# Four cached tiles of DSA per transfer, and one transposed-probability tile for two heads, in a two-layer streaming encoder step

## The chip, the cores and the metric

The kernel runs on one NeuronCore of a Trainium2 chip. The metric is device time in microseconds, the median of 3 runs. Times inside a run come from one profiled execution; a time such as 1469.76 is microseconds from that execution's first instruction.

Engines are called as in the profile: PE (matrix multiply), DVE (vector), ACT (scalar), POOL (GpSimd), SP (it issues nearly all loads and stores here). Each engine works through its own list in order and waits on semaphores of the others.

## The reference

Two layers of a streaming encoder, for a prompt of 512 rows and 8 running streams of 16 rows (640 rows, f32). Two of a layer's four branches are attention, and only those are touched:

```python
def mla_attend(q_pos, qb, k, v, k_pos):            # branch A, 4 heads
    s = jnp.einsum('bqhd,bshd->bhqs', qb, k).astype(F32) * A_SCALE
    s = jnp.where(vis[None, None], s, -jnp.inf)
    p = jax.nn.softmax(s, axis=-1).astype(v.dtype)
    return jnp.einsum('bhqs,bshd->bqhd', p, v)

def dsa_attend(...):                               # branch B, 4 heads
    _, sel = lax.top_k(iscore, topk)               # an indexer chooses the keys
    logits = jnp.einsum('bqhd,bqkhd->bqhk', qb, k_sel).astype(F32) * B_SCALE
    logits = logits + jnp.moveaxis(bias, -1, 2)
    p = jax.nn.softmax(logits, axis=-1).astype(v.dtype)
    return jnp.einsum('bqhk,bqkhd->bqhd', p, v_sel)
```

The streams attend over 512 cached rows each beside their own 16. The cached keys and values of branch B come as `c_bkT` (2 layers, 4 heads, 4 tiles of 128 x 512) and `c_bv` (2 layers, 2 head pairs, 8 streams, 128 x 512); a tile is 256 KB.

## The kernel before

**Order.** The code is written as a plain sequence. A scheduler that estimates when each operation can start sets the order on every engine at build time; on the chip that order is fixed. So between the small matmuls of attention stand matmuls of the gate projections (lines 117 to 119, 128 x 320 each, three to a product), which depend on no attention and fill PE.

**Attention of the prompt.** One unit is a block of 128 queries (`qt` 0 to 3) and a pair of heads. `mla_front` and `dsa_front` make scores and softmax and leave `P`, one tile for each head. `mla_back` and `dsa_back` turn `P`: `transposed` puts up to four 128 x 128 blocks of one head into a PSUM bank (line 680) and copies the bank to an SBUF tile `PT` with `cp`, which takes ACT and DVE in turn (lines 96, 98). Then `pv` (line 728) multiplies with the values: for each key block one matmul for each of the two heads. The two heads write PSUM rows 0 to 63 and 64 to 127 and use two different 64-column groups of the PE array (`tile_position=(0, 64 * hf)`). There are 80 of these in MLA and 80 in DSA over both layers, 160 in all. `piped` lets the fronts run two units ahead of the backs.

**Attention of the streams in DSA.** `dsas_front(h)` loads four tiles of `c_bkT`, each into a buffer of its own (`cache()`, tag `ca`, 4 buffers, shared with other uses), and makes one score matmul from each (line 916), each on its own 32-column group and 32 PSUM rows (`tile_position=(0, 32 * p)`): 32 over both layers. `dsas_back` does the values for two heads: for each half of the streams (`g` 0 and 1) four tiles of `c_bv` (tag `cd`, 4 buffers) and 16 matmuls (line 952) that go round the four 32-column groups: 128 over both layers. Line 935 transposes, line 942 is the product with the streams' own rows.

**Loads.** SP issues all these loads in its own fixed order, with the gate weights (`wst`, 512 KB each) among them. A load waits in that list until its buffer is free, and all that stands behind it waits too.

A matmul of f32 operands shows as two rows in the trace, a transposition or a projection matmul as one.

Of the kernel before, what the change touches and what calls it, by code (L numbers as in the profile page):

```python
# [22 lines left out]
NT = 5  # L23
NJ = 22
REG = 3
DFF = 2816
ALPHA = (2 * L) ** 0.25
EPS = 1e-5
# [227 lines left out]
def layer(tc, l, I, O, E):  # L256
# [4 lines left out]
    xh, xl, ident = E["xh"], E["xl"], E["ident"]  # L261
# [31 lines left out]
    def cache():  # L293
        return mk(at, "ca", 512, 4)
# [400 lines left out]
    def pt(nm, p, n, w=T):  # L695
        return mk(p, nm, w, n)

    def piped(units, front, back, lag):
        held = []
        for u in units:  # L700
            held.append((u, front(*u)))
            if len(held) > lag:
                v, r = held.pop(0)
                back(*v, r)
        for v, r in held:
            back(*v, r)
# [14 lines left out]
            out.append(P)  # L721
        return out

    def pv(po, PTs, v, n, h0):
        for kb in range(n):
            for hf, PT in enumerate(PTs):
                o = kb * 256 + 64 * (h0 + hf)
                pe.matmul(po[64 * hf : 64 * hf + 64], lhsT=v[:, o : o + 64], rhs=PT[:, kb * 128 : kb * 128 + 128],  # L728
                          start=kb == 0, stop=kb == n - 1, tile_position=(0, 64 * hf))

    def mla_back(qt, k, Ps):
        PTs = [transposed(P, qt + 1, pt("PT", m2, 3, 512)) for P in Ps]
        if k == 0:
            mla[qt] = aps()
        po = mla[qt][:, k * 128 : k * 128 + 128]
        pv(po, PTs, va, qt + 1, 2 * k)
        split_out(0, k, slice(qt * 128, qt * 128 + 128), po)
# [168 lines left out]
    def dsas_front(h):  # L906
        k, hf = h // 2, h % 2
        ns = slice(64 * hf, 64 * hf + 64)
        cb = mk(ds, "cb", T, 2)
        sp.dma_start(cb, biasS[h])  # L910
        pool.tensor_tensor(cb, cb, wk[3], op=ALU.add)
        ps, pn = aps(), aps()[:, 0:128]
        for p in range(4):
            c_ = cache()
            sp.dma_start(c_, I["c_bkT"][l, h, p])
            pe.matmul(ps[32 * p : 32 * p + 32, :], lhsT=db[:, h * 128 + 32 * p : h * 128 + 32 * p + 32], rhs=c_,  # L916
                      start=True, stop=True, tile_position=(0, 32 * p))
        pe.matmul(pn, lhsT=bq[k][ns], rhs=bk[k][ns], start=True, stop=True)
        P = pt("P", ds, 4)
        sm = col()  # L920
        dsa_soft([(ps, 512), (pn, 128)], cb, P, sm)
        norm(P, T, sm)
        return P

    def dsas_back(h, P):
        k, hf = h // 2, h % 2
        if hf == 0:
            dsa["s", k] = mk(ds, "PT2", 5 * 256, 1)
        PT = dsa["s", k]
        PTv = PT.rearrange("p (b s f q) -> p b s f q", b=5, s=NS, f=2)  # L930
        for b in range(5):
            if b % 4 == 0:
                ps = aps()
            tp = ps[:, (b % 4) * 128 : (b % 4) * 128 + 128]
            pe.transpose(tp, P[:, b * 128 : b * 128 + 128], ident)
            cp(PTv[:, b, :, hf], s3(tp))
        if hf == 0:
            return
        pr = aps()[:, 0:256]
        for g in range(2):  # L940
            pg_ = pr[:, g * 128 : g * 128 + 128]
            pe.matmul(pg_, lhsT=PT[:, 1024 + g * 128 : 1152 + g * 128], rhs=bv[:, 1024 + k * 128 : 1152 + k * 128],
                      start=True, stop=False)
            cs_ = []
            for i in range(4):
                c_ = mk(ds, "cd", 512, 4)
                sp.dma_start(c_, I["c_bv"][l, k, 4 * g + i])
                cs_.append(c_)
            for kb in range(4):
                for i, c_ in enumerate(cs_):  # L950
                    o = kb * 256 + g * 128 + i * 32
                    pe.matmul(pg_[32 * i : 32 * i + 32], lhsT=PT[:, o : o + 32], rhs=c_[:, kb * 128 : kb * 128 + 128],
                              start=False, stop=kb == 3, tile_position=(0, 32 * i))
        pc_ = mk(ds, "cb", T, 2)[:, 0:256]
        act.copy(pc_, pr)
        po = aps()[:, 0:256]
        for g in range(2):
            pe.transpose(po[:, g * 128 : g * 128 + 128], pc_[:, g * 128 : g * 128 + 128], ident)
        pov = po.rearrange("p (s f q) -> p s f q", s=NS, f=2)
        for f in range(2):  # L960
            rows = slice(64 * f, 64 * f + 64)
            hi = s3(bh[1][k][rows, TP:T])
            act.copy(hi, pov[rows, :, f])
            dve.tensor_sub(s3(bl[1][k][rows, TP:T]), pov[rows, :, f], hi.bitcast(F32))
# [32 lines left out]
        return out  # L997

    def dsa_back(k, qt, Ps):
        PTs = [transposed(P, qt + 1, pt("PT", ds, 4, 512)) for P in Ps]  # L1000
        if qt == 0:
            dsa[k] = aps()
        pv(dsa[k][:, qt * 128 : qt * 128 + 128], PTs, bv, qt + 1, 2 * k)
        if qt == 3:
            split_out(1, k, slice(0, TP), dsa[k])
# [465 lines left out]
```

## Time and profile before

| | |
|---|---|
| median of 3 runs | 2123.42 us (2122.09 to 2124.9) |
| the profiled execution | 2131.17 us, of which its span from first to last instruction 2128.8 us |
| PE busy | 2069.5 us, 97% of the span |
| DVE, ACT, POOL busy | 72%, 43%, 22% |
| chain of work that ended last | PE 80%, DVE 7%, DMA 5% |

The page has the busy time of each engine, the span in 40 slices, the queues, and the chain followed back from the last instruction. A matmul's time from start to end overlaps with the next one's; what a matmul costs PE is the step from its start to the next start.

Attention and the projections between stand at about 257 to 505 us (layer 0) and 1307 to 1564 us (layer 1) of the span.

### The profile page before, as it was taken

The page shows a single profiled execution, that of the slowest core. Times are in us where ns is not written, and L with a number is a line of the kernel's source. Part 1 is how long each engine was busy: PE and PEld are TensorE (multiplying, and loading weights), DVE is VectorE, ACT ScalarE, POOL GpSimd, SP SyncE. Part 2 cuts the span into 40 slices and gives each one's busy share as a digit, 9 for nine tenths or more (in the row PEclk, how much of TensorE's full clock was granted, in tenths as well). Part 3 has the DMA queues.
Part 4 walks back from the last instruction along what each step waited for, and adds up shares of the span by engine and source line. Part 5 has one row for each costly group of instructions (what it writes and reads, how often), then busy time and mean ns, then how long its engine had stood idle before and what let it go on. Part 6 is the DMA issues. An engine that isn't in the chain of part 4 may idle for free.

```text
span 2128.8 us, 33842 instructions
## 1 busy us (share of the span) xinstructions
PE 2069.5 (97%) x12828; PEld 1863.3 (88%) x12828; DVE 1533.4 (72%) x2775; ACT 913.8 (43%) x1682; POOL 459.6 (22%) x709
## 2 busy tenths in 40 slices
PE   6999999999999999999899999999999999999997
PEld 6998979779989899989699999797898899899995
DVE  6999994633389778766679989945334899679657
ACT  5433432322256545544434334333232566555543
POOL 2200001411114323322302000023110143323222
PEclk9999999999999999999999999999999999999999
DMA  8452225432443544542653522254324344525525
GB/s 275 105 166 85 75 72 162 136 126 80 144 141 112 117 106 103 129 120 70 175 144 82 171 64 71 92 166 132 107 85 150 136 123 120 128 89 140 129 54 152
DMA packets 137882, 257.22 MB, mean 121 GB/s; under 512 B 33068, under 2 KB 53328, under 8 KB 137200
## 3 DMA queue, kind: packets, MB, share of 16 engines
q1 hardware_dynamic: 121880, 223.61, 33.0%
q0 software_dynamic: 15840, 31.46, 8.7%
q8 instruction: 101, 1.65, 0.3%
q14 instruction: 61, 0.50, 0.1%
HBM read 202.06 MB, written 52.96 MB: 120 GB/s over the span
## 4 chain that ended last, share of the span: by engine, by line
PE 80%; DVE 7%; DMA 5%; issue 4%; ACT 3%; POOL 2%; SPq 0%; DVEq 0%; POOLq 0%; ACTq 0%
PE g L118 18%; PE g L117 18%; PE g L119 18%; PE a L117 5%; PE a L118 5%; PE a L119 5%; PE a L728 1%; PE a L680 1%; DVE wl L113 1%; DVE uac L1218 1%; PE a L916 1%; DMA wst<-in_wd 1%; PE a L715 1%; ACT wh L111 1%; DMA wst<-in_wo 1%
## 5 line engine op out<-in xcount | busy, mean ns | idle before, releaser
L117 PE MATMUL g<-xh,wh 128*128 128x320 f32 x1568 | 493.8, 316 | 4.3 <-ACT xh L174 1.8
L118 PE MATMUL g<-xl,wh 128*128 128x320 f32 x1568 | 490.1, 313 | 1.6 <-DVE xl L175 1.6
L119 PE MATMUL g<-xh,wl 128*128 128x320 f32 x1568 | 489.3, 312 | 0.0
L117 PEld LDWEIGHTS g<-xh,wh 128*128 128x128 f32 x1568 | 295.5, 189 | 15.4 <-issue 6.8
L118 PEld LDWEIGHTS g<-xl,wh 128*128 128x128 f32 x1568 | 295.7, 189 | 8.9 <-issue 5.6
L119 PEld LDWEIGHTS g<-xh,wl 128*128 128x128 f32 x1568 | 295.6, 189 | 7.2 <-issue 7.0
L111 ACT CAST wh<-wst 128x1024 fp32r<-128x1024 f32 (+1 forms) x168 | 174.7, 1040 | 258.7 <-PE g L118 131.7
L113 DVE TENSOR_TENSOR wl<-wst,wh 128x1024 fp32r<-128x1024 f32 (+1 forms) x168 | 204.7, 1219 | 69.6 <-ACT wh L111 60.2
L118 PE MATMUL a<-wl,hh 128*128 128x512 f32 x544 | 216.0, 397 | 1.1 <-DVE wl L113 1.1
L117 PE MATMUL a<-wh,hh 128*128 128x512 f32 x544 | 214.0, 398 | 0.6 <-ACT hh L1230 0.4
L119 PE MATMUL a<-wh,hl 128*128 128x512 f32 x544 | 213.3, 396 | 0.0
L1218 DVE SCALAR_TENSOR_TENSOR uac<-ext,pc,uac 128x656 f32<-128x656 f32 (+2 forms) x184 | 152.2, 867 | 6.0 <-ACT uac L1215 5.6
L119 PE MATMUL g<-xh,sl 128*128 128x320 f32 x456 | 140.6, 309 | 3.9 <-DVE sl L1145 3.9
L117 PE MATMUL g<-xh,sh 128*128 128x320 f32 x456 | 140.9, 309 | 1.4 <-ACT sn L1183 0.9
L118 PE MATMUL g<-xl,sh 128*128 128x320 f32 x456 | 140.7, 309 | 0.0
L854 POOL TENSOR_TENSOR acx<-acx,gt 128x640 f32<-128x640 f32 x32 | 52.5, 1640 | 390.1 <-DVE gt L845 317.7
L845 DVE SCALAR_TENSOR_TENSOR gt<-gt,g 128x320 f32<-128x320 f32 x96 | 46.3, 484 | 125.1 <-ACT wh L111 92.7
L117 PEld LDWEIGHTS a<-wh,hh 128*128 128x128 f32 x544 | 102.3, 188 | 24.9 <-ACT hh L1230 1.2
L119 PEld LDWEIGHTS a<-wh,hl 128*128 128x128 f32 x544 | 102.5, 188 | 24.4
L118 PEld LDWEIGHTS a<-wl,hh 128*128 128x128 f32 x544 | 102.4, 188 | 23.9 <-DVE wl L113 1.8
L1144 ACT CAST sh<-acx 128x1024 fp32r<-128x1024 f32 (+1 forms) x80 | 75.5, 944 | 77.0 <-PE g L118 56.7
L1144 ACT CAST sh<-sg 128x1024 fp32r<-128x1024 f32 (+1 forms) x72 | 67.8, 942 | 89.9 <-PE g L118 85.2
(399 smaller groups left out, 4858.5 us busy)
## 6 DMA issues: line engine op xcount, KB each, us to landing
wst<-in_wg SPq DMA_DIRECT2D x64, 512.0 KB, 3.5
wst<-in_wd SPq DMA_DIRECT2D x44, 512.0 KB, 6.7
acx<-in_ws SPq DMA_DIRECT2D x40, 512.0 KB, 4.2
sg<-in_ws SPq DMA_DIRECT2D x36, 512.0 KB, 5.5
xa<-acx POOLq DMA_DIRECT2D x60, 256.0 KB, 6.0
wst<-in_wa SPq DMA_DIRECT2D x22, 512.0 KB, 3.7
xa<-dn POOLq DMA_DIRECT2D x40, 256.0 KB, 8.7
wbs<-in_wb SPq DMA_DIRECT2D x64, 128.0 KB, 2.6
```

The costliest lines, as they stand in the source:

```text
L111: act.copy(wh[:, :cols], st[:, :cols])
L113: dve.tensor_sub(wl[:, :cols], st[:, :cols], wh[:, :cols].bitcast(F32))
L117: pe.matmul(ps, lhsT=ah, rhs=bh, start=first, stop=False, skip_group_check=more)
L118: pe.matmul(ps, lhsT=ah, rhs=bl, start=False, stop=False, skip_group_check=more)
L119: pe.matmul(ps, lhsT=al, rhs=bh, start=False, stop=last, skip_group_check=more)
L680: pe.transpose(ps[:, b * 128 : b * 128 + 128], P[:, (b0 + b) * 128 : (b0 + b) * 128 + 128], ident)
L715: pe.matmul(ps, lhsT=qh[h][0:100, qt * 128 : qt * 128 + 128], rhs=kT[0:100, h * 512 : h * 512 + W], start=True, stop=True)
L728: pe.matmul(po[64 * hf : 64 * hf + 64], lhsT=v[:, o : o + 64], rhs=PT[:, kb * 128 : kb * 128 + 128], start=kb == 0, stop=kb == n - 1, tile ...
L845: dve.scalar_tensor_tensor(dst[:, a:b], g_[:, a:b], 1.0, ps, op0=ALU.add, op1=ALU.mult)
L854: pool.tensor_tensor(acc[m], acc[m], g_, op=ALU.add)
L1144: act.copy(sh, sg[:, a : a + n])
L1218: dve.scalar_tensor_tensor(ac[:, a:b], ext[:, i + a : i + b], wc[i], ac[:, a:b], op0=ALU.mult, op1=ALU.add)
```

## The change

Three edits:

- `dsas_front` loads the four `c_bkT` tiles of a head with one transfer of 1 MB into a tile `c4` of 2048 columns, and `dsas_back` the four `c_bv` tiles of a half in the same way. Both take turns in one pair of `c4` buffers; `cd` and its four buffers are gone. SP issues 48 transfers fewer (64 become 16).
- `transposed2` puts the blocks of both heads, one after the other for each key block, into one tile `PT2h` of 1024 columns (2 buffers), four blocks to a bank and a copy. It takes the place of the two calls of `transposed` in `mla_back` and `dsa_back`. ACT and DVE each have 8 copies fewer over both layers.
- `pv` reads both heads from that tile. Its matmuls are as many as before.

PE has the same matmuls as before, in another order between the start of MLA and the end of DSA of each layer; its list outside these stretches is the same.

```diff
+C4 = 2
+    def transposed2(Ps, n, p, bufs):
+        PT = mk(p, "PT2h", 1024, bufs)
+        for b0 in range(0, 2 * n, 4):
+            nb = min(4, 2 * n - b0)
+            ps = aps()
+            for b in range(nb):
+                kb, hf = divmod(b0 + b, 2)
+                pe.transpose(ps[:, b * 128 : b * 128 + 128], Ps[hf][:, kb * 128 : kb * 128 + 128], ident)
+            cp(PT[:, b0 * 128 : (b0 + nb) * 128], ps[:, : nb * 128])
+        return PT
...
-    def pv(po, PTs, v, n, h0):
+    def pv(po, PT, v, n, h0):
         for kb in range(n):
-            for hf, PT in enumerate(PTs):
+            for hf in range(2):
                 o = kb * 256 + 64 * (h0 + hf)
-                pe.matmul(po[64 * hf : 64 * hf + 64], lhsT=v[:, o : o + 64], rhs=PT[:, kb * 128 : kb * 128 + 128],
+                c = (2 * kb + hf) * 128
+                pe.matmul(po[64 * hf : 64 * hf + 64], lhsT=v[:, o : o + 64], rhs=PT[:, c : c + 128],
                           start=kb == 0, stop=kb == n - 1, tile_position=(0, 64 * hf))
...
-        PTs = [transposed(P, qt + 1, pt("PT", m2, 3, 512)) for P in Ps]
+        PTs = transposed2(Ps, qt + 1, m2, 2)
...
+        c4 = mk(ds, "c4", 2048, C4)
+        sp.dma_start(c4.rearrange("q (p n) -> q p n", p=4), I["c_bkT"][l, h].rearrange("p q n -> q p n"))
         for p in range(4):
-            c_ = cache()
-            sp.dma_start(c_, I["c_bkT"][l, h, p])
-            pe.matmul(ps[32 * p : 32 * p + 32, :], lhsT=db[:, h * 128 + 32 * p : h * 128 + 32 * p + 32], rhs=c_,
+            pe.matmul(ps[32 * p : 32 * p + 32, :], lhsT=db[:, h * 128 + 32 * p : h * 128 + 32 * p + 32],
+                      rhs=c4[:, p * 512 : p * 512 + 512],
                       start=True, stop=True, tile_position=(0, 32 * p))
...
-            cs_ = []
-            for i in range(4):
-                c_ = mk(ds, "cd", 512, 4)
-                sp.dma_start(c_, I["c_bv"][l, k, 4 * g + i])
-                cs_.append(c_)
+            c4 = mk(ds, "c4", 2048, C4)
+            sp.dma_start(c4.rearrange("q (i n) -> q i n", i=4),
+                         I["c_bv"][l, k, 4 * g : 4 * g + 4].rearrange("i q n -> q i n"))
+            cs_ = [c4[:, i * 512 : i * 512 + 512] for i in range(4)]
...
-        PTs = [transposed(P, qt + 1, pt("PT", ds, 4, 512)) for P in Ps]
+        PTs = transposed2(Ps, qt + 1, ds, 2)
```

In what follows, line numbers in the pieces of the changed order are its own: 706 is the transposition (680 before), 741 the product with the values (728), 929 the score of the streams (916), 118 to 120 the projections (117 to 119). Names are the tiles' names with a running number; `c_` is `c4`.

PE, layer 0, the scores of the third stream head, with the values of a prompt unit and the transpositions of another head between; before:

```order
L916 MATMUL a_4702<-ca_4704,db_4256 32x512
L117 MATMUL g_5262<-xh,wh_5258 128x320
L918 MATMUL a_4703<-bk_810_4248,bq_809_4246 128x128
L118 MATMUL g_5262<-xl,wh_5258 128x320
L916 MATMUL a_4702<-ca_4707,db_4256 32x512
L728 MATMUL a_4556<-PT_4675,bv_4250 64x128
L728 MATMUL a_4556<-PT_4682,bv_4250 64x128
L728 MATMUL a_4556<-PT_4675,bv_4250 64x128
L728 MATMUL a_4556<-PT_4682,bv_4250 64x128
```

The same head in the changed order:

```order
L118 MATMUL g_5289<-xh,wh_5260 128x320
L119 MATMUL g_5289<-xl,wh_5260 128x320
L929 MATMUL a_4658<-c_955_4660,db_4240 32x512 x4
L932 MATMUL a_4659<-bk_798_4232,bq_797_4230 128x128
L120 MATMUL g_5289<-xh,wl_5262 128x320
```

The four scores of the head, each apart before, now follow each other.

PE, layer 1, the values of a prompt unit of MLA with two key blocks; before:

```order
L715 MATMUL a_13135<-kT_11492,qh_2086_12053 128x384
L728 MATMUL a_13098<-PT_13123,va_13000 64x128
L715 MATMUL a_13145<-kT_11492,qh_2087_12054 128x384
L118 MATMUL g_14298<-bl_2211_12759,wbh_14294 128x320
L728 MATMUL a_13098<-PT_13127,va_13000 64x128
L680 MATMUL a_13156<-ident,P_13074 128x128 x2
L680 MATMUL a_13161<-ident,P_13084 128x128 x2
```

The same unit in the changed order:

```order
L727 MATMUL a_13059<-kT_11412,qh_2039_11974 128x384
L741 MATMUL a_13015<-PT2h_13040,va_12920 64x128 x2
L706 MATMUL a_13070<-ident,P_12994 128x128
L706 MATMUL a_13070<-ident,P_13004 128x128
L706 MATMUL a_13070<-ident,P_12994 128x128
L706 MATMUL a_13070<-ident,P_13004 128x128
```

The two heads' products, apart before, now stand side by side, and the four transpositions of the next unit go to one bank.

SP, layer 0, loads of `c4` (`in_c_bkT`, `in_c_bv`), of the bias rows (`cb`) and of gate weights (`wst`) in the changed order; before, the 256 KB loads of `ca` and `cd` stood in their place in fours:

```order
L110 DMA wst_5602<-in_wg 128x1024
L927 DMA c_955_4660<-in_c_bkT 128x4x512
L923 DMA cb_4569<-biasS 128x640
L923 DMA cb_4609<-biasS 128x640
L927 DMA c_967_4696<-in_c_bkT 128x4x512
L923 DMA cb_4655<-biasS 128x640
L923 DMA cb_4691<-biasS 128x640
L959 DMA c_976_4728<-in_c_bv 128x4x512
L110 DMA wst_5688<-in_wg 128x1024
L959 DMA c_977_4747<-in_c_bv 128x4x512
```

The third and later `c4` loads of a layer wait for the matmuls of the load two before, and weights stand behind them.

## Rows read from the trace of the kernel before

**Rows 1.** The page: PE's busy time; the chain that ended last, by engine.

```profile
PE 2069.5 (97%) x12828; PEld 1863.3 (88%) x12828; DVE 1533.4 (72%) x2775; ACT 913.8 (43%) x1682; POOL 459.6 (22%) x709
PE 80%; DVE 7%; DMA 5%; issue 4%; ACT 3%; POOL 2%; SPq 0%; DVEq 0%; POOLq 0%; ACTq 0%
```

**Rows 2.** Stretches: length, busy us by engine (instructions), granted clock, DMA share, GB/s.

```profile
250.00:300.00 50.00, 50.00 (x319) 41.28 (x318) 46.45 (x122) 18.90 (x56) 4.99 (x3) 1.00 0.21 64
...
400.00:450.00 50.00, 50.00 (x310) 33.92 (x309) 28.87 (x71) 17.96 (x43) 14.15 (x10) 1.00 0.44 136
...
1300.00:1350.00 50.00, 50.00 (x311) 40.56 (x309) 46.01 (x122) 19.89 (x57) 3.22 (x2) 1.00 0.17 56
...
1450.00:1500.00 50.00, 50.00 (x289) 32.68 (x287) 25.14 (x68) 16.65 (x38) 14.92 (x11) 1.00 0.44 138
```

**Rows 3.** PE's waits: whom for, us in total, times, longest.

```profile
PE a L171 <- DVE z L162: 16.2, 3, 11.1
...
PE a L952 <- DMA cd<-in_c_bv: 1.7, 2, 1.4
```

**Rows 4.** PE in order of time, layer 1, DSA: start, us, instruction, trace rows merged.

```profile
1469.16 0.31 PE L117 MATMUL g<-bh,wbh 128*128 128x320 f32 x1
1469.40 0.43 PE L728 MATMUL a<-PT,bv 128*64 128x128 f32 x2
1469.76 1.06 PE L916 MATMUL a<-ca,db 128*32 128x512 f32 x8
1470.75 0.49 PE L918 MATMUL a<-bk,bq 64*128 64x128 f32 x2
...
1471.43 0.65 PE L728 MATMUL a<-PT,bv 128*64 128x128 f32 x6
1472.01 0.77 PE L680 MATMUL a<-ident,P 128*128 128x128 f32 x5
1472.53 0.39 PE L118 MATMUL g<-bl,wbh 128*128 128x320 f32 x1
1472.77 0.31 PE L119 MATMUL g<-bh,wbl 128*128 128x320 f32 x1
1472.91 0.31 PE L117 MATMUL g<-bh,wbh 128*128 128x320 f32 x1
...
1476.16 1.04 PE L916 MATMUL a<-ca,db 128*32 128x512 f32 x2
1477.13 0.48 PE L918 MATMUL a<-bk,bq 64*128 64x128 f32 x2
```

**Rows 5.** PE in order of time, layer 0, values of the streams (idle before, releaser).

```profile
460.61 0.41 PE L952 MATMUL a<-cd,PT 128*32 128x128 f32 x2 [1.44 <-DMA cd<-in_c_bv]
...
464.56 0.41 PE L952 MATMUL a<-cd,PT 128*32 128x128 f32 x2
464.90 0.42 PE L118 MATMUL g<-xl,wh 128*128 128x320 f32 x1
...
465.69 1.06 PE L952 MATMUL a<-cd,PT 128*32 128x128 f32 x26
466.68 0.42 PE L119 MATMUL g<-xh,wl 128*128 128x320 f32 x1
```

**Rows 6.** Loads: tile, queue, count, KB each, median us from issue to landing.

```profile
cd<-in_c_bv SPq DMA_DIRECT2D x32, 256.0 KB, 3.5
ca<-in_c_bkT SPq DMA_DIRECT2D x32, 256.0 KB, 4.9
...
gb<-in_ln SPq DMA_DIRECT2D x2, 1024.0 KB, 6.3
```

**Rows 7.** The DVE half of the copies: duration ns min/median/max, first and last start.

```profile
L98 DVE COPY PT<-a x56: 273/354/692, 256.5 to 1537.7; 128x128 f32<-128x128 f32 x28, 128x512 f32<-128x512 f32 x12, 128x256 f32<-128x256 f32 x8, 128x384 f32<-128x384 f32 x8
```

**Rows 8.** PE alone, stretches in layer 0: length, busy (instructions), clock, DMA.

```profile
371.80:374.90 3.10, 3.10 (x12) 0.99 1.04 306
374.90:378.30 3.40, 3.40 (x13) 0.50 0.71 233
```

## The prediction

> **What bounds the kernel now.** I read the page's busy times and chain first: PE is busy for 2069.5 us of the 2128.8 us span and makes 80% of the chain that ended last [rows 1]. Shares of a whole span can hide a stage with another limit, so I read the stretches that hold the touched code next: in four such stretches of 50 us PE is busy for all 50, with DVE at 46 us in the MLA stretches (250 to 300, 1300 to 1350) and at 25 to 29 us in the DSA stretches [rows 2]. Then PE's waits: the longest are for layer norms, elsewhere (line 171); of the touched code only the loads of `cd` stand in the list, 1.7 us in all [rows 3]. So in these stretches PE always has its next instruction ready, and the time there is the sum of PE's steps from start to start. Copies, loads and issues that the change saves lie beside that and are worth nothing by themselves. What counts is how much the same matmuls cost PE in the changed order.
>
> They don't cost the same, as the start times show. A lone score matmul of line 916 takes 0.97 us (1476.16 to 1477.13); four that follow each other, on four column groups, take 0.99 us together (1469.76 to 1470.75) [rows 4]. So three of the four are all but free when nothing stands between them. Line 728 behaves likewise with its two column groups: a lone matmul 0.36 us (1469.40 to 1469.76), three 0.58 us (1471.43 to 1472.01) [rows 4]; so a run costs about 0.15 us and 0.22 us for each pair or lone remainder. Line 952: one 0.34 us, thirteen 0.99 us [rows 5]. And each excursion from the projections to other matmuls costs on both sides: the step into it 0.24 us (1469.16 to 1469.40) and the first step after it 0.24 us (1472.53 to 1472.77), where projections step by 0.14 to 0.15 us [rows 4], so about 0.09 us twice.
>
> **The change part by part.** I count runs in the two orders: a run is a row of matmuls of one line with nothing else on PE between. The sum is made against the profiled execution (2131.17 us, span 2128.8 us); it is 7.8 us or 0.4% above the median, which changes a difference of 30 us by 0.1 us, so I take the difference off the median.
>
> *Scores of the streams (line 916).* Before, 32 matmuls in 24 runs (19 of one); after, 32 in 10 runs (6 of four, 2 of three, 2 of one), since one transfer frees all four at once. 14 runs fewer at 0.97 to 0.99 us: **13.7 us**. All in DSA.
>
> *Values of the prompt (line 728).* Before, 160 in 52 runs, 40 of them odd, so 100 pair places; after, 38 runs, none odd, 80 pair places, because a copy now brings both heads. 20 x 0.22 + 14 x 0.15 = **6.5 us**, of which 11 places and 7 runs, 3.5 us, in MLA.
>
> *Values of the streams (line 952).* 9 runs of one, 2 of two and 1 of three go, 12 x 0.34 = 4.1 us. One run of four comes, and four runs of 13 become 16. From one to thirteen a further matmul costs (0.99 - 0.34) / 12 = 0.054 us: 0.5 + 12 x 0.054 = 1.15 us come back. Net 3.0 us. The wait for `cd`, 1.7 us (its longest part stands at 460.61 [rows 5]), ends as well, if the new loads are in time (below). Together **4.7 us**.
>
> *Excursions.* 149 before, 120 after, over both layers; all 29 fewer are in DSA. At 0.18 us each they are worth 5.2 us; into a transposition the step is often no longer than between projections, so the lower bound is the way out alone, 2.6 us. I take **4.0 us**.
>
> *Transpositions (line 680)*: as many, in somewhat fewer runs; nothing taken. *16 copies fewer*, 0.27 to 0.69 us each by width [rows 7]: half on ACT and half on DVE, both hidden behind PE. Nothing, except as DVE's reserve in MLA. *48 issues fewer on SP*: nothing, SP only waits for buffers there.
>
> Sum: 13.7 + 6.5 + 4.7 + 4.0 = 28.9 us.
>
> *What may come late next.* DVE has only 3.5 to 4 us of idle time in each MLA stretch [rows 2], and its work there, the top-k search above all, does not shrink. So I take half of MLA's 3.5 us back: 1.8 us. In DSA its busy share is little over half.
>
> *The new loads.* No transfer of 1 MB with 2 KB rows stands in the trace. Its bounds: the 1024 KB load of `gb` lands 6.3 us after its issue; four `ca` loads one after the other without overlap would take 4 x 4.9 = 19.6 us [rows 6]. I take 6.3 us, the load of the same size. The time it has, from the last matmul on the buffer to the first on the new data, I add up from the PE steps of the changed order: 8.9, 9.1 and 9.4 us for the three tightest of the 12 reloads, 13.2 us on average. At 6.3 us none is late. In SP's list gate weights stand behind these waiting loads, but their first use is 40 us or more behind, by the same steps.
>
> *The shared bank.* A prompt unit's values now wait for a copy of up to 512 columns with both heads, up to 0.69 us, where a copy of 128 columns takes 0.27 us [rows 7]. Between a unit's last transposition and its first product the changed order has at least 14 projections, 2.1 us. So the copy is hidden, with about a microsecond to spare at the tightest place.
>
> Forecast: 28.9 - 1.8 = 27.1 us less, 2123.4 - 27.1 = **2096 us**.
>
> **The rivals.**
>
> *Hand-offs take the place of idle matmuls.* A faster PE reaches each dependent step earlier. If each of the 32 prompt units waits for a copy or a softmax by half of the widest copy, 0.35 us, 11 us come back: 2107 us. For it: the spare microsecond above, DVE at 46 of 50 us in MLA. Against: the trace has no such wait on PE today [rows 3], and in most units more projections stand between.
>
> *The clock.* At 374.9 to 378.3 PE ran at a granted clock of 0.50, 1.2 GHz, with 13 instructions started, right behind a stretch of small score matmuls without a projection, though PE showed as busy throughout [rows 8]. The changed order packs small matmuls closer. If 12 such falls of 3.4 us come anew, each loses 1.7 us: 20 us, 2116 us. Against: the longest stretches without projections are as long before as after. The Trainium skill, "TensorE: Matmul & The Clock Gate", Part 1: The HAM clock gate, says that the throttled state is the default and activity releases it; by that rule denser packing of thin matmuls speaks against this change. The trace shows one such fall in the attention stretches of both layers, so it agrees only weakly.
>
> *The change doesn't do what it says*: what sets the start and end of DSA is not PE but a chain through DVE's top-k, the softmaxes and the hand-offs, so that PE only gets holes where it had lone matmuls: 2123 us. Against: PE full in the stretches [rows 2].
>
> *Slower: the big loads are late.* There are two `c4` buffers for keys and values together, and SP waits in order. If 1 MB lands like four single loads one by one, in 19.6 us, each of the 12 reloads is 6.4 us late on average against its 13.2 us. Two loads are under way at a time, and a wait for one serves the other, so about half counts: 38 us, 2096 + 38 = 2134 us. It decides from about 18 us of landing time on (27 us lost, 12 x 4.5 / 2). For it: DMA is at 0.44 in DSA [rows 2]. Against: the 6.3 us of `gb`.
>
> **How the numbers follow.** Forecast 0.70, hand-offs 0.13 (2107), clock 0.05 (2116), no effect 0.05 (2123), late loads 0.07 (2134). The predicted time is the forecast's. Downwards the terms could be larger by the excursions' upper bound (1.2 us), MLA's share kept (1.8 us) and some 5 us of clock falls that a shift in time may spare (three like the one above): 2088 us. Upwards the range takes in the hand-offs with some room: 2110 us. Outside are the last three rivals, 0.17. A measurement of this kernel can tell 0.2%, some 4 us, from no change. Faster by more than that are the first three cases, 0.88; within it the fourth, 0.05; slower the last, 0.07.
>
> **What would show it.** Right: line 916's four in 0.99 us in most places, line 728 never in odd runs, both DSA stages shorter by about 12 us and both MLA stages by 1 to 2 us, the rest of the span unchanged, and no wait of PE for `c4`. Wrong: rows of PE waiting for `c4`, for `PT2h` or for `P`; idle time in slices that were full; a granted clock under 1 in DSA; or a DSA stage as long as before with holes on PE.

## The result, and the profile of the changed kernel

The changed kernel takes 2093.1 us (median of 4 runs, 2092.74 to 2094.82). Before, beside it, takes 2123.65 us. The ratio is 0.9858, with a 95% interval of 0.9841 to 0.9875: 30.5 us less, where 27.1 us less (2096 us) were predicted. The execution that was profiled took 2094.82 us; its span is 2092.7 us.

The lines that answer [rows 1], PE's busy time and the chain by engine. PE has lost 33.5 us of busy time and still fills 97% of the span:

```profile
PE 2036.0 (97%) x12828; PEld 1854.5 (89%) x12828; DVE 1530.0 (73%) x2767; ACT 911.5 (44%) x1674; POOL 455.3 (22%) x709
...
PE 81%; DVE 6%; issue 5%; DMA 4%; ACT 2%; POOL 2%; SPq 0%; POOLq 0%; DVEq 0%; ACTq 0%
```

The four stretches of [rows 2] (length, busy us by engine with instructions, granted clock, DMA share, GB/s):

```profile
250.00:300.00 50.00, 50.00 (x328) 42.77 (x327) 48.66 (x123) 20.21 (x58) 5.02 (x3) 1.00 0.19 64
400.00:450.00 50.00, 50.00 (x355) 40.33 (x356) 31.27 (x82) 18.68 (x44) 18.32 (x13) 1.00 0.37 130
1300.00:1350.00 50.00, 50.00 (x341) 39.05 (x341) 49.20 (x116) 19.72 (x53) 4.68 (x3) 1.00 0.23 77
1450.00:1500.00 50.00, 50.00 (x392) 39.79 (x389) 26.42 (x70) 17.05 (x40) 15.68 (x10) 1.00 0.52 176
```

PE is full in all four, as before, but starts more instructions in the same 50 us: 392 in place of 289 in the last. DVE is now at 48.7 and 49.2 us of 50 in the MLA stretches, and PE still doesn't wait for it. The list of PE's waits, the answer to [rows 3], begins and ends as follows; `c4`, `PT2h` and `P` are not in it:

```profile
PE a L172 <- DVE z L163: 16.0, 3, 10.8
...
PE g L118 <- ACT gt L842: 0.5, 1, 0.5
```

What PE does in a prompt unit of DSA, layer 1, beside [rows 4] (start, us, instruction; the trace has two rows for an FP32 matmul, so x8 is four):

```profile
1465.93 0.31 PE L120 MATMUL g<-bh,wbl 128*128 128x320 f32 x1
1466.17 0.66 PE L741 MATMUL a<-PT2h,bv 128*64 128x128 f32 x8
1466.76 1.07 PE L929 MATMUL a<-c,db 128*32 128x512 f32 x8
1467.75 0.44 PE L741 MATMUL a<-PT2h,bv 128*64 128x128 f32 x4
1468.12 0.49 PE L932 MATMUL a<-bk,bq 64*128 64x128 f32 x2
```

Four prompt products take 0.59 us (1466.17 to 1466.76), where three took 0.58, and four stream scores take 0.99 us (1466.76 to 1467.75), where before a lone one took 0.97. The stream values, beside [rows 5]:

```profile
1495.12 0.43 PE L965 MATMUL a<-c,PT 128*32 128x128 f32 x8
1495.48 0.49 PE L956 MATMUL a<-bv,PT 128*128 128x128 f32 x2
1495.90 1.08 PE L965 MATMUL a<-c,PT 128*32 128x128 f32 x32
1496.91 0.42 PE L120 MATMUL g<-bh,wbl 128*128 128x320 f32 x1
```

Four take 0.36 us and sixteen 1.01 us, where one took 0.34. The new loads, beside [rows 6] (the tile is called `c` in the views; its one landing that the trace resolves is 5.5 us), and the copies into the shared tile on both engines, beside [rows 7] (ns min/median/max, first and last start):

```profile
c<-in_c_bv SPq DMA_DIRECT2D x8, 1024.0 KB, 5.5
```

```profile
L99 DVE COPY PT2h<-a x24: 402/680/693, 259.0 to 1471.3; 128x512 f32<-128x512 f32 x16, 128x256 f32<-128x256 f32 x8
L97 ACT COPY PT2h<-a x24: 362/586/589, 262.7 to 1469.2; 128x512 f32<-128x512 f32 x16, 128x256 f32<-128x256 f32 x8
```

**By stretch.** The order of PE's instructions outside attention is the same in both kernels, so the span can be cut at the same matmuls, by their start times in the trace. In us, with the time at a granted clock of 0.50 inside a stretch in brackets:

| | to MLA 0 | MLA 0 | DSA 0 | between | MLA 1 | DSA 1 | rest |
|---|---|---|---|---|---|---|---|
| before | 243.5 | 110.3 | 140.6 (3.4) | 796.5 (27.3) | 113.2 | 149.1 | 553.4 |
| after | 245.1 (3.4) | 108.5 | 126.8 | 790.9 (17.1) | 109.8 | 134.1 | 554.8 (3.4) |

The attention stages shrink from 513.2 to 479.2 us. The falls of the clock don't stand where they stood. This is before, at 1214.5 us, and then after in the same stretch (columns as above):

```profile
1214.50:1224.70 10.20, 10.20 (x35) 8.52 (x34) 8.88 (x23) 1.79 (x3) 0.00 (x0) 0.50 0.39 129
```

```profile
89.10:92.50 3.40, 3.40 (x16) 3.29 (x15) 3.40 (x10) 2.26 (x6) 2.01 (x6) 0.50 0.65 193
1214.50:1224.70 10.20, 10.20 (x64) 8.37 (x65) 9.62 (x29) 2.24 (x6) 0.98 (x2) 1.00 0.35 117
```

Before, this stretch ran at half the clock (1.2 GHz), with 35 instructions started on PE; after, it runs at the whole clock, with 64 (the work there is some 15 to 20 us further on). Outside attention PE's order is the same, and of the 2.6 us by which the two profiled executions differ there, 1.7 are the clock. Below, "net" is a time less half of the time at half clock inside it. Attention, net: **511.5 us before, 479.2 after, 32.3 less**.

### The profile page after: what moved, and what is told of

Its sections match the earlier page's. It is cut to its first block, busy times and chain, and to the rows that moved or that the text cites. A ratio compares the mean times of both kernels' runs of the same rounds, so it can differ in the third digit from the quotient of the medians.

```text
span 2092.7 us, 33730 instructions
## 1 busy us (share of the span) xinstructions
PE 2036.0 (97%) x12828; PEld 1854.5 (89%) x12828; DVE 1530.0 (73%) x2767; ACT 911.5 (44%) x1674; POOL 455.3 (22%) x709
## 4 chain that ended last, share of the span: by engine, by line
PE 81%; DVE 6%; issue 5%; DMA 4%; ACT 2%; POOL 2%; SPq 0%; POOLq 0%; DVEq 0%; ACTq 0%
PE g L119 18%; PE g L120 18%; PE g L118 18%; PE a L118 5%; PE a L119 5%; PE a L120 5%; PE a L741 1%; DMA wst<-in_wo 1%; PE a L706 1%; DVE wl L114 1%; PE a L727 1%; DVE uac L1231 1%; DVE acx L163 1%; DMA wst<-in_ws 1%; ACT wh L112 1%
## 5 line engine op out<-in xcount | busy, mean ns | idle before, releaser
L120 PE MATMUL g<-xh,sl 128*128 128x320 f32 x456 | 140.6, 309 | 3.9 <-DVE sl L1158 3.9
```

Source lines behind the costliest of these rows:

```text
L120: pe.matmul(ps, lhsT=al, rhs=bh, start=False, stop=last, skip_group_check=more)
```

## The experiments

Each kernel was timed beside the kernel before on its own chip. Attention is the sum of the four stages, net, in the profiled execution; "elsewhere" is the other three stretches, net. In e2 and e6 a few matmuls of attention stand behind the end of layer 0's DSA stage as cut above; these two are read at a later cut, where all attention is done in every kernel, as a difference from before.

| kernel | median us (before there) | ratio, 95% interval | attention | elsewhere |
|---|---|---|---|---|
| before | 2123.65 | | 511.5 | 1579.8 |
| after | 2093.1 (2123.65) | 0.9858, 0.9841 to 0.9875 | 479.2 | 1578.9 |
| e1_loads_only | 2103.74 (2125.62) | 0.9890, 0.9866 to 0.9914 | 487.0 | 1580.3 |
| e2_share_only | 2117.94 (2125.62) | 0.9963, 0.9947 to 0.9978 | 502.4 | 1582.6 |
| e3_pv_by_head | 2103.21 (2125.62) | 0.9885, 0.9864 to 0.9906 | 486.2 | 1582.5 |
| e4_four_transfers | 2104.9 (2125.62) | 0.9902, 0.9878 to 0.9926 | 478.6 | 1588.3 |
| after_again | 2094.33 (2125.78) | 0.9849, 0.9829 to 0.9869 | 479.2 | 1581.1 |
| e5_two_transfers | 2094.08 (2125.78) | 0.9851, 0.9830 to 0.9872 | 479.4 | 1581.2 |
| e7_stream_share | 2089.67 (2125.78) | 0.9822, 0.9803 to 0.9841 | 476.1 | 1578.4 |
| e9_share_and_rows | 2081.11 (2125.78) | 0.9800, 0.9774 to 0.9825 | 468.6 | 1579.6 |
| e10_copy_per_block | 2122.8 (2128.81) | 0.9977, 0.9959 to 0.9994 | 507.6 | 1579.3 |
| e8_bv_by_stream | 2099.39 (2128.81) | 0.9878, 0.9850 to 0.9905 | 491.7 | 1575.3 |
| e6_one_buffer | 2093.53 (2128.81) | 0.9842, 0.9811 to 0.9873 | 482.8 | 1575.7 |

The theory: PE's order alone makes the gain; a run of matmuls pays once for entering and leaving it, and what shares the array inside the run is nearly free. The rivals: the gain lies in fewer transfers, issues and copies; or the switch between kinds of matmul costs, and not the place on the array.

**The two parts apart.** The loads alone, against before:

```diff
-            c_ = cache()
-            sp.dma_start(c_, I["c_bkT"][l, h, p])
+        c4 = mk(ds, "c4", 2048, C4)
+        sp.dma_start(c4.rearrange("q (p n) -> q p n", p=4), I["c_bkT"][l, h].rearrange("p q n -> q p n"))
...
-                c_ = mk(ds, "cd", 512, 4)
-                sp.dma_start(c_, I["c_bv"][l, k, 4 * g + i])
+            c4 = mk(ds, "c4", 2048, C4)
+            sp.dma_start(c4.rearrange("q (i n) -> q i n", i=4),
+                         I["c_bv"][l, k, 4 * g : 4 * g + 4].rearrange("i q n -> q i n"))
```

> The kernel before with the loads alone changed: c4 for cached keys and values, the probabilities still transposed head by head. Its order has line 916's matmuls in 9 runs (24 before), line 952's in 21 (31), line 728's in 52 as before, and 18 excursions from the projections fewer. Theory (the time is the sum of PE's steps, so a run fewer is its step saved): 15 x 0.98 + 4.5 for line 952 and its wait + 18 x 0.16 = 22 us less than before, 2101 to 2103 us. Rival (the gain comes from the shared tile, copies and banks): within 5 us of before.

And the shared tile alone, against before:

```diff
-        PTs = [transposed(P, qt + 1, pt("PT", m2, 3, 512)) for P in Ps]
+        PTs = transposed2(Ps, qt + 1, m2, 2)
...
-        PTs = [transposed(P, qt + 1, pt("PT", ds, 4, 512)) for P in Ps]
+        PTs = transposed2(Ps, qt + 1, ds, 2)
```

> The kernel before with the shared probability tile alone, the loads as before. Its order has line 728's matmuls in 38 runs, none odd (52, 40 odd), line 916's in 22 (24), and 8 excursions fewer. Theory: 5.7 to 6.5 + 2 x 0.98 + 8 x 0.16 = 9 us less than before, 2114 to 2116 us; with the loads alone it adds up to the whole change. Rival (the shared tile carries the gain): 2100 us or less. Rival (copies and hand-offs of two heads cost what the pairs gain): 2123 us.

Measured: 2103.74 and 2117.94 us, 22 and 8 us under before, both close to what was expected. In attention the loads save 24.5 us and the shared tile 9.1 us, together 33.6 where the whole change saves 32.3: two parts that nearly add. The 1.4 us by which e2's total falls short of its attention stand elsewhere (see e4).

**Heads apart.** The changed kernel, with one head's products before the other's:

```diff
-        for kb in range(n):
-            for hf in range(2):
+        for hf in range(2):
+            for kb in range(n):
```

> The changed kernel with the products of the values in another order inside a unit: all key blocks of one head, then all of the other, where the heads alternate in the changed kernel. The same matmuls, in as many runs (38). Theory (matmuls overlap only with a neighbour on another column group): in a run of n only the two in the middle overlap, so 122 places where 80 were, 42 x 0.22 = 9 us more than the changed kernel, 2101 to 2104 us. Rival (what costs is the switch from one kind of matmul to another, not the neighbour's column group): as the changed kernel, 2093 us.

Eight products now take 1.51 us (445.12 to 446.63); in the changed kernel a run of eight takes 1.03 us (442.94 to 443.97). e3, and behind it the changed kernel:

```profile
445.12 1.58 PE L741 MATMUL a<-PT2h,bv 128*64 128x128 f32 x16
446.63 0.44 PE L949 MATMUL a<-ident,P 128*128 128x128 f32 x2
```

```profile
442.94 1.09 PE L741 MATMUL a<-PT2h,bv 128*64 128x128 f32 x16
443.97 0.44 PE L949 MATMUL a<-ident,P 128*128 128x128 f32 x2
```

The total, 2103.21 us, is in the theory's range; by the ratios it is 6 to 8 us above the changed kernel. The line itself grew by 5.6 us (22.9 to 28.5) where 9 were expected, since the order that was built mixes the heads again in places; with its surroundings attention grew by 7.0 us. It speaks against the rival: the copies, transfers and sharing are those of the changed kernel.

**The number of transfers.** The changed kernel, each `c4` filled by four transfers:

```diff
-        sp.dma_start(c4.rearrange("q (p n) -> q p n", p=4), I["c_bkT"][l, h].rearrange("p q n -> q p n"))
+        for p in range(4):
+            sp.dma_start(c4[:, p * 512 : p * 512 + 512], I["c_bkT"][l, h, p])
...
-            sp.dma_start(c4.rearrange("q (i n) -> q i n", i=4),
-                         I["c_bv"][l, k, 4 * g : 4 * g + 4].rearrange("i q n -> q i n"))
+            for i in range(4):
+                sp.dma_start(c4[:, i * 512 : i * 512 + 512], I["c_bv"][l, k, 4 * g + i])
```

> The changed kernel with each c4 tile filled by four transfers of 256 KB in place of one of 1 MB; tiles, buffers and the runs on PE stay (3 excursions more). Theory (only PE's order counts, issues and transfers are hidden): 2092 to 2096 us. Rival (the single transfer itself brings something): 48 issues at 0.44 us on the path, up to 21 us more than the changed kernel, 2105 to 2114 us.

By its total, 2104.9 us, the rival was right. By stretch it wasn't: attention takes 478.6 us, as in the changed kernel, and the loss stands in the rest of layer 1, 564.6 us in place of 554.8. There the built order of the feed-forward part differs from the changed kernel's, though nothing was edited in it. Two things in the profile answer for most of the 9.8 us. PE waits 9.0 us for line 1159 there, where the changed kernel waits 3.9 us for the same step, and 10.2 us at half clock in place of 3.4 cost 3.4 us more. PE's waits in e4:

```profile
PE g L120 <- DVE sl L1159: 9.0, 2, 4.6
```

So this kernel changed two things. With two transfers of 512 KB the built order on PE is the changed kernel's outside DSA of layer 0. There (436 to 490 us) the two traces differ, against what was expected: some projections stand in other places, while the lines that the change touches have as many runs. This kernel was run beside the changed kernel itself:

```diff
-        sp.dma_start(c4.rearrange("q (p n) -> q p n", p=4), I["c_bkT"][l, h].rearrange("p q n -> q p n"))
+        for p in (0, 2):
+            sp.dma_start(c4[:, p * 512 : p * 512 + 1024].rearrange("q (p n) -> q p n", p=2),
+                         I["c_bkT"][l, h, p : p + 2].rearrange("p q n -> q p n"))
```

(the values alike)

> The changed kernel itself, beside the three below on one chip. Its lines answer for the run-to-run spread: 0.984 to 0.9875 of before, about 2093 us, with attention stretches that sum to 479 us less any clock fall. Where the falls of the granted clock stand need not repeat.

> The changed kernel with each c4 filled by two transfers of 512 KB in place of one of 1 MB (keys and values alike). TensorE's order of instructions is that of the changed kernel through the whole program, which it was not with four transfers (e4). Theory: TensorE's order alone makes the gain, so the time is the changed kernel's within 4 us (about 2093). Rival: issues on SP and the shape of the transfers carry part of the gain; e4's total was 10 us worse with 48 issues more, so 16 more should cost a third of that, 3 to 4 us, and they should stand in the DSA stretches or behind them, as waits for SP's loads.

2094.08 us beside 2094.33, attention 479.4 beside 479.2 us. In layer 1, where the order of attention is the same from instruction to instruction in the changed kernel, e4 and e5, it takes 244.0 us in all three. More issues and another shape of transfer cost nothing that can be measured. The Trainium skill, "DMA: Bandwidth & Descriptors", Measured, advises to batch transfers to 1 MiB or more, for the sake of bandwidth; here that size by itself bought no time, because PE waits for no load at either size. What the single transfer gave was that four matmuls became ready at once, and a shared buffer that several transfers fill does so as well.

**Late loads.** The changed kernel with one `c4` buffer:

```diff
-C4 = 2
+C4 = 1
```

> The changed kernel with one c4 buffer in place of two, so that each of 14 reloads starts only when the last matmul on the block before it is done. TensorE has 31 to 57 instructions, roughly 5 to 10 us, between the two. Theory: a 1 MB load lands in about 5.5 us, as in the changed kernel; then at most the tightest wait by a microsecond or two, and the DSA stages are longer by under 3 us each (a run or two more for the stream scores). Rival (the late loads of the prediction): a load lands like four single ones after each other, near 19.6 us; then most reloads hold TensorE up by about 10 us, waits for c stand at the head of TensorE's list, and the DSA stages grow by tens of us. The built order also differs in layer 0's feed-forward part, which may move the total by some 10 us.

Of 14 reloads one makes PE wait, for 1.0 us (PE in order of time, idle before and its releaser):

```profile
488.06 0.31 PE L120 MATMUL g<-bh,wbl 128*128 128x320 f32 x1
489.32 0.75 PE L965 MATMUL a<-c,PT 128*32 128x128 f32 x19 [0.96 <-DMA c<-in_c_bv]
```

Attention grows by 3.5 us, and the total stays, since the stretch between the layers' attention is shorter in the order that was built here. Late loads, the slower rival of the prediction, were far away: even one buffer all but sufficed. Nor does the gain come from room for more loads: before, `ca` and `cd` held eight tiles, two `c4` hold eight too, and one holds four.

**The copies.** The changed kernel with one copy for each block of 128 columns, tile and bank shared as before:

```diff
-            cp(PT[:, b0 * 128 : (b0 + nb) * 128], ps[:, : nb * 128])
+            for c in range(0, nb):
+                cp(PT[:, (b0 + c) * 128 : (b0 + c + 1) * 128], ps[:, c * 128 : c * 128 + 128])
```

> The changed kernel with one copy for each transposed block of 128 columns (both heads still share one PT2h tile and one bank). Theory: the wide copy earns its gain by what it makes of TensorE's order, since four blocks become ready together. With narrow copies the built order has line 741's 160 matmuls in 102 runs with 124 pair places, where the changed kernel has 38 runs and 80 places; at 0.15 us for a run and 0.22 us for a pair place that is 64 x 0.15 + 44 x 0.22 = 19 us, and 37 excursions more at 0.14 to 0.18 us are 5 to 7 us: attention stretches of about 504 us in place of 479, about 2118 us in all. The order outside attention is the same. Rival: the shared tile alone matters, copies and their number lie beside TensorE's work, and the time stays at 2093 us.

2122.8 us: 28.4 us of attention are lost again, all but 4 of what the whole change brought. Line 742 (741 of the changed kernel) costs 41.7 us in place of 22.9, 18.8 more where 19 were expected; the steps out of and into the projections cost 9 us more where 5 to 7 were expected, so that attention is 507.6 us where about 504 were. What it looks like on PE, MLA of layer 1:

```profile
1329.36 0.66 PE L706 MATMUL a<-ident,P 128*128 128x128 f32 x4
1329.78 0.39 PE L119 MATMUL g<-bl,wbh 128*128 128x320 f32 x1
1330.01 0.31 PE L120 MATMUL g<-bh,wbl 128*128 128x320 f32 x1
1330.24 0.43 PE L742 MATMUL a<-PT2h,va 128*64 128x128 f32 x2
1330.61 0.44 PE L706 MATMUL a<-ident,P 128*128 128x128 f32 x2
```

A product goes out alone as soon as its block is copied: 0.37 us for one (1330.24 to 1330.61) where four cost 0.59. With narrow copies the shared tile is worse than none at all: beside e1, which has the new loads and separate tiles with wide copies, attention is 20.6 us longer. So the copies matter greatly, but not for the time that they take on DVE and ACT, since no wait for `PT2h` stands in PE's list here either: they set what becomes ready together, and with that PE's order.

**Place or switch.** The changed kernel with the loops of the stream values exchanged:

```diff
-            for kb in range(4):
-                for i, c_ in enumerate(cs_):
+            for i, c_ in enumerate(cs_):
+                for kb in range(4):
```

> The changed kernel with the loops of the streams' values exchanged: the four key blocks of one stream in a row (one column group), then the next stream. The same matmuls, loads and copies. Theory: matmuls cost little only when their neighbour is on another column group. A pass on one group steps by 109 ns, and an FP32 matmul makes two, so 12 runs of one, 4 of thirteen and 4 of sixteen cost 12 x 0.34 + 4 x 2.9 + 4 x 3.6 = 30 us in place of 9.7 us on that line: the DSA stages longer by about 10 us each, about 2113 us in all. Rival: only the switch from one kind of matmul to another costs; then line 965 stays near 9.7 us and DSA as it is. The built order also differs in layer 0's feed-forward part, so that the total may be off by some 10 us; the DSA stages and the line decide.

Sixteen matmuls, the same ones in another order, take 2.39 us (465.31 to 467.70) where they took 1.01:

```profile
465.31 2.46 PE L965 MATMUL a<-c,PT 128*32 128x128 f32 x32
467.70 0.42 PE L119 MATMUL g<-xl,wh 128*128 128x320 f32 x1
```

Line 965 costs 21.3 us in place of 9.7. That settles place against switch: the runs still number 20. It isn't the adding up of four products in one place either: transpositions, each into columns of its own, step by the same 109 ns. But the size was 11.6 us more and not 20. The trace shows why: within a stream the passes step by 109 ns, as assumed, but where one stream hands over to the next their passes interleave, at 30 and 79 ns. Attention is 12.5 us longer, the total only some 6 us by the ratios (0.9878 beside 0.9849 of after_again), because the stretch between the layers' attention is shorter in the order built here, as in e6.

**One step further.** If runs and places are what costs, more of both can be had. e7 transposes the streams' probabilities of both heads together:

```diff
-            pe.transpose(tp, P[:, b * 128 : b * 128 + 128], ident)
-            cp(PTv[:, b, :, hf], s3(tp))
+            for f in range(2):
+                pe.transpose(ps[:, c + f * 128 : c + f * 128 + 128], Ps[f][:, b * 128 : b * 128 + 128], ident)
+            cp(PTv[:, b], ps[:, c : c + 256].rearrange("p (f s q) -> p s f q", f=2, s=NS))
```

> The changed kernel, and in addition the streams' probabilities of both heads are transposed together, one key block of both heads to a copy (5 copies of 256 columns in place of 10 of 128). By TensorE's order: 358 steps out of the projections in place of 372, stream values in 12 runs in place of 20. Theory (a run pays once for each switch): 14 excursions less at 0.24 us (6.9 us over 29, as the change measured) are 3.4 us, and 8 runs fewer on the stream values at 0.14 us (0.356 for four, 1.010 for sixteen) 1.1 us: 4 to 5 us under the changed kernel, about 2088 us. With the predicted 0.14 us for an excursion it would be 3 us. Rival: the second head's softmax now holds up the first head's transposes, TensorE waits for P in the list of waits, and the time is the changed kernel's or worse (2093 to 2100).

2089.67 us, 4.7 under the changed kernel beside it. In attention it is 3.1 us: 1.1 on line 966, as expected, and 1.75 on the projections' side where 3.4 were expected, which is 0.125 us for each of 14 excursions. Nearly all that went began with a transposition, into which the step is 0.15 us, no longer than between projections; into a product it is 0.24.

e9 adds the order of the DSA prompt scores:

```diff
         for hf in range(2):
+            q_, kh_, kl_ = dsa["qk", hf]
+            pe.matmul(pss[hf], lhsT=q_[:, qt * 128 : qt * 128 + 128], rhs=kh_[:, 0:W], start=True, stop=False)
+        for hf in range(2):
...
-            pe.matmul(ps, lhsT=q_[:, qt * 128 : qt * 128 + 128], rhs=kh_[:, 0:W], start=True, stop=False)
-            pe.matmul(ps, lhsT=q_[ns, qt * 128 : qt * 128 + 128], rhs=kl_[ns, 0:W], start=False, stop=True,
+            pe.matmul(pss[hf], lhsT=q_[ns, qt * 128 : qt * 128 + 128], rhs=kl_[ns, 0:W], start=False, stop=True,
```

> e7, and in addition the prompt scores of a DSA pair are issued as two full matmuls and then the two that use only 64 rows (the two low parts, each on its own half of the rows). In the changed kernel a half-row matmul costs TensorE as much as a full one of the same width: 0.31 us for 256 columns, 0.37 for 384, 0.43 for 512. Theory: halves on different rows run beside each other as column groups do; four pairs of each width over both layers then save up to 4 x (0.15 + 0.31 + 0.37 + 0.43) = 5 us on that line, about 2083 us in all. Rival: only column groups run beside each other, and the line costs what it did: as e7, within 2 us.

**2081.11 us, ratio 0.9800 (0.9774 to 0.9825)**: 13.2 us under the changed kernel on the same chip, and the best of all. The changed kernel and e9 in the same unit, 512 columns:

```profile
393.08 0.49 PE L997 MATMUL a<-dkh,dq 128*128 128x512 f32 x1
393.51 0.50 PE L998 MATMUL a<-dkl,dq 64*128 64x512 f32 x1
393.94 0.50 PE L997 MATMUL a<-dkh,dq 128*128 128x512 f32 x1
394.37 0.49 PE L998 MATMUL a<-dkl,dq 64*128 64x512 f32 x1
394.79 0.66 PE L706 MATMUL a<-ident,P 128*128 128x128 f32 x4
```

```profile
391.13 0.73 PE L997 MATMUL a<-dkh,dq 128*128 128x512 f32 x2
391.80 0.50 PE L1001 MATMUL a<-dkl,dq 64*128 64x512 f32 x2
392.22 0.66 PE L706 MATMUL a<-ident,P 128*128 128x128 f32 x4
```

The two half-row matmuls take 0.42 us together, where each took 0.43, and the four 1.09 us in place of 1.71. Over both layers the two lines cost 14.6 us in place of 21.1, 6.5 less where at most 5 were expected: the two full ones, side by side, also take less, 0.67 us (391.13 to 391.80), where each took 0.43 with a half-row one behind it. The second half starts 3 to 4 ns after the first in the trace. The Trainium skill, "TensorE: Matmul & The Clock Gate", Part 3: Packing small matmuls — row/col tiling, says that matmuls on different parts of the array start some 4 ns apart; the trace agrees on halves of the rows (3 to 4 ns) and shows 6 to 7 ns on column groups.

## Why the prediction was right, step by step

It was right in mechanism, in sign and nearly in size (2096 against 2093.1, range 2088 to 2110); by its terms the gain was taken somewhat too small. These are the terms, from the start times of PE in the two profiled executions:

| term | predicted us | measured us |
|---|---|---|
| scores of the streams, 24 to 10 runs | 13.7 | 13.6 (23.5 to 9.9) |
| values of the prompt, 52 to 38 runs | 6.5 | 5.7 (28.6 to 22.9) |
| values of the streams, 31 to 20 runs | 3.0 | 4.7 (14.4 to 9.7) |
| waits for `cd` | 1.7 | 1.6 |
| excursions, 29 fewer | 4.0 | 5.3, about 3 of it at lone projections |
| scores of MLA (line 715, now 727) | 0 | 1.7 (16.0 to 14.4) |
| transpositions | 0 | 0.4 |
| DVE takes back in MLA | -1.8 | 0 |
| sum | 27.1 | 33.0 |

The terms add to 33.0 us beside the 32.3 us that attention lost net; 0.7 us is left unassigned. The medians differ by 30.5 us. The 2 us between these two lie within what a measurement can tell, and the profiled execution of before was not the typical one.

- *PE is the bound, and time is the sum of its steps*: right. The stretches stay full, copies and issues are worth nothing in themselves (e5), and the loss in e3, e8 and e10 is PE's own.
- *Values of the streams*: undersized. The step said that one run of four brings back 0.50 us and that growing from 13 to 16 costs 0.054 us a matmul. Four take 0.36 us, hardly more than one, and sixteen 1.01 beside thirteen at 0.99: with four column groups in turn, a full set costs hardly more than its first member does. That is 0.7 us. The other 1.0 lay before the change: I took two runs of two at little more than a lone one, but they took 0.98 us (460.61 to 461.59) and 0.78 us (1546.08 to 1546.85), since the second matmul came only when the first was over, in one of them because of its load:

```profile
461.25 0.41 PE L952 MATMUL a<-cd,PT 128*32 128x128 f32 x2 [0.24 <-DMA cd<-in_c_bv]
```

- *Excursions*: undersized. I took 0.14 us each (4.0 over 29). They gave 5.3, which is 0.18 each, the upper of the prediction's two prices. Before, sixteen projections stood alone between two pieces of attention, after only two; nine of the sixteen stood beside a stream score. Such a step, mostly of 0.32 to 0.34 us, pays for both sides at once, where projections step by 0.15. Before, layer 0:

```profile
413.99 0.41 PE L119 MATMUL g<-xh,wl 128*128 128x320 f32 x1
414.33 1.04 PE L916 MATMUL a<-ca,db 128*32 128x512 f32 x2
```

  e7 gave 0.125 us, for excursions that mostly began with a transposition and so paid on the way out alone. The price depends on what begins the excursion; the prediction knew that and took a middle value.
- *Scores of MLA (line 715)*: the forecast had no term for them, and their own steps fell by 1.7 us; somewhat over half of it is real. A product starts only when the matmul before it is all but done, 0.07 us before the end that the trace models for it: 0.24 us after a projection of 0.31 us, and 0.74 us after a score of MLA that is 0.81 us long. Before, layer 0 (start, us, instruction), and behind it the same place after:

```profile
266.46 0.81 PE L715 MATMUL a<-kT,qh 100*128 100x384 f32 x2
267.20 0.44 PE L728 MATMUL a<-PT,va 128*64 128x128 f32 x4
```

```profile
264.14 0.81 PE L727 MATMUL a<-kT,qh 100*128 100x384 f32 x2
264.49 0.61 PE L120 MATMUL g<-xh,wl 128*128 128x320 f32 x1
264.93 0.31 PE L118 MATMUL g<-xh,wh 128*128 128x320 f32 x1
```

  A projection behind the same score starts after 0.35 us, but then steps 0.44 us itself (264.49 to 264.93) in place of 0.15. So the score costs 0.64 us there, and the product behind it adds 0.10, about what it adds behind a projection (0.09): the price does not depend on what runs just ahead. Of the 32 scores eight had a product right behind before, and two after. The projections right behind scores gave 0.7 of the 1.7 us back; that stands in the table as a smaller saving of the excursions. The Trainium skill, "TensorEngine Tiling (Array Packing)", Key Properties, says that a change of tiling mode drains TensorE; the trace agrees, with the product's late start. But that is not all of the price, since the step out of a transposition, which uses the whole array, is 0.23 us too.
- *Hand-offs, the likeliest rival*: no wait of PE on a copy or a softmax came in attention, so nothing of its 11 us.
- *Half of MLA's gain back to DVE*: wrong. DVE had 3.5 to 4 us of room in 50 and used 2.2 to 3.2 of it. MLA became 1.8 and 3.4 us shorter, where 1 to 2 us each were expected. A busy share of 46 of 50 was no bound, because no step of PE hung on its last part.
- *Loads and the shared bank*: right. A landing of 5.5 us against 6.3 taken and 8.9 us to spare; no wait for `c4` or `PT2h`. e6 shows how much margin was there.
- *DSA shorter by about 12 us each*: 13.8 us (12.1 net) and 15.0 us.
- *The rest of the span unchanged*: right for PE's order, and nearly so in time: elsewhere 1579.8 and 1578.9 us net.
- *The clock*: attention of the changed kernel had no fall in this execution. Over all seven stretches there were 30.7 us at half clock before and 23.9 us after, in other places. e9, the densest, has 13.7 us. That denser packing costs clock is not borne out by these runs.

## What to carry to other kernels

Where TensorE is full, count its runs: matmuls that use part of the array cost little only while the neighbour in the order uses another part, and a lone one pays for the whole (here 0.97 us for one stream score and 0.99 for four). Make what belongs side by side become ready together (one buffer, one wide copy for a full set); the number of transfers and the time of the copies are secondary, and sharing a tile without the wide copy can lose what it was meant to gain. Compare kernels stage by stage, since an edit can change the scheduler's order far behind it and move the total by some 10 us, as in e4.

## What was not expected

- The built order of the feed-forward part turned over with edits in attention that touch nothing there (e2, e4, e6, e8). With the turn in layer 1 the last stretch took 563.0 and 564.6 us (e2, e4) in place of 553 to 556; with the turn in layer 0 the stretch between took about 778 us net (e2, e6, e8), where the other kernels have 781 to 785. Whether it is this turn alone was not tried by itself.
- The same program has its falls of the clock in other places from one execution to the next. The changed kernel had 3.4 us at half clock at 89 us and none in DSA in one execution, and in the other none there and 3.4 us at 1421 us, right in DSA of layer 1. Nothing in its order had changed, so a single fall in a stage is no trait of a kernel.
- One stream after the other costs 2.39 us for sixteen matmuls and not the 3.6 that 109 ns a pass would make, since the passes of neighbouring streams interleave where they meet.
